# Normalised rows of the value stage transposed in 32 by 32 blocks on VectorE and kept by token tile, their residual added by an accumulating transfer

## The chip, the cores and the metric

The kernel runs on one core of a Trainium2 chip. The metric is the device time in microseconds of one execution.

The engines are TensorE (PE, matmuls; PEld is its weight load), VectorE (DVE), ScalarE (ACT), GpSimd (POOL) and SyncE (SP). SP issues the plain transfers between DRAM and the on-chip memory (SBUF); POOL issues those that add into what they write. Matmul results land in PSUM, which has eight banks.

## The reference

One layer of a streaming encoder over 2048 tokens of width 1024, all in float32. Each sub-layer normalises its input, and its output again before the residual sum:

```
u = rms_norm(h, g_mix_pre);   z = u @ w_in
y = concat(window_attention(z), gated_recurrence(z)) @ w_out
h = h + rms_norm(y, g_mix_post)
u = rms_norm(h, g_x_pre);     m = rms_norm(mem, g_mem)
y = cross_attention(u, m, wq_x, wk_x, wv_x) @ wo_x        # 4 heads, 256 memory tokens
h = h + rms_norm(y, g_x_post)
u = rms_norm(h, g_ffn_pre)
y = (silu(u @ w_gate) * (u @ w_up)) @ w_down              # inner width 2816
h = h + rms_norm(y, g_ffn_post)
```

The change is at the seam of the last two sub-layers: the second `h`, its norm, and the hand-over of `u` to the feed-forward.

## The kernel before

Float32 products are made of three passes in a rounded format: each operand is split into a high part (a copy by ACT, L997) and a low part (the rest, by DVE, L1000), and PE multiplies high by high, high by low and low by high (L1141 to L1143).

From about 740 us on the work is a list of jobs: the output projection (mixed stage), attention scores (score stage), values (value stage), gate and up projections for the first and the second 1024 tokens (feed-forward), and the down projection (down stage). Each job has blocks, each block two row tiles of 128 rows by 1024 columns of result. A block is done by Strassen's scheme in seven steps instead of eight; a step (`products`) is 12 matmuls of 128 by 128 by 512. Its moving operands are the T tiles: one for each of seven combinations of the weight's quarters, resident for a whole job, 128 by 2 (high, low) by 4 contraction tiles by 512. Seven slots hold them, so at the change from one job to the next each slot is refilled as its last user of the old job ends. Its stationary operands are the S tiles, formed for each block two steps ahead from `sraw` loads. In the feed-forward the roles are such that the activations `u` are the T tiles and the weights are streamed.

T tiles are made in halves by `resident`: a row tile is loaded, and `split2` writes its high and low parts. Where a combination of quarters is needed, it was formed before and stored to DRAM (`u0_s` for the first 1024 tokens, `u_s` for the second).

What follows a block's products is its tail, a generator (`after`) of which one piece runs with each step of the following blocks; the pieces are given in program order, and each engine works through its own queue in an order that a planner fixes at build time from simulated times. An engine that waits holds up all that is queued behind it. The mixed and score stages' tails hand their rows on by `blocked` and `store_blocked`: DVE transposes 32 by 32 blocks, and four stores put the quarters at their places in DRAM.

The value stage's tail (`value_block`, L1620) of the kernel before: root mean square of each row (ACT squares, POOL), scaling (L1640), the add of the `h1` rows that SP had loaded (L1644), the store of the sum, squares again (L1516), scaling (L1653); then `transposed` (L1394): eight PE transposes of 128 by 128 into two PSUM banks (L1402), copied out by ACT (L1403), and one store to `u_d`, which is laid out by contraction tile. For row tiles 4 to 7 the tiles 0 to 3 are read back and combined with them into `u0_s` by `token_sums` (L1441).

Of the kernel before, what the change touches and what calls it, by code (L numbers as in the profile page):

```python
# [18 lines left out]
P = 128  # L19
T = 2048  # L20
# [28 lines left out]
class Layer:  # L49
# [111 lines left out]
    def run(self):  # L161
# [13 lines left out]
        self.vo_d = tc.dram_tile([D, D], F32, name="vo_d")  # L175
        self.u_d = tc.dram_tile([KT, P, T], F32, name="u_d")
        self.h_d = tc.dram_tile([NFF, P, T], F32, name="hid_d")
# [288 lines left out]
    def in_first(self):  # L466
# [65 lines left out]
        def fetch():  # L532
            for s in range(2):
                for q in range(2):
# [11 lines left out]
                  for i, p in enumerate(self.ORDER)]  # L546
# [3 lines left out]
                      + [("v", lambda kind: iter([None]), out, after, keep) for _, out, after, keep in plain])  # L550
        phases = self.phases([(lambda i, j, a, n: raw[i, j][:, a:a + n, :], 4, blocks, None, {})], T)
        PE, ACT, DVE, POOL = (getattr(mybir.EngineType, e) for e in ("PE", "Activation", "DVE", "Pool"))
# [450 lines left out]

    def resident(self, get, nk, key, dst, keep, sums):

# [18 lines left out]
        def split(a, b, t, o):  # L1024
            if o is not None:
                nc.vector.tensor_tensor(t, t, o, ALU.add if key == 6 else ALU.subtract)
            self.split2(t, dst[:, 0, a:b], dst[:, 1, a:b], "A")

# [200 lines left out]
    def phases(self, jobs, first, prologue=None):  # L1229
# [51 lines left out]
        def half(g, tile):  # L1281

            if current[0] is None:
                if not queue:
                    return False
                free = min(slots, key=lambda s: s[1])
                if free[1] > g:
                    return False
                n, p, _ = k = queue.pop(0)
                slots.remove(free)  # L1290
                slots.append((free[0], uses[k][-1], free[2]))
                self._n += 1
# [5 lines left out]
                current[:] = [(k, self.resident(fetch(n, tile), jobs[n][1], p, dst, keep[n], jobs[n][3] is not None)), 0]  # L1298
            k, f = current[0]
# [52 lines left out]
        fresh = False  # L1352
        for _, nk, bl, _, beside in jobs:
            for i, (kind, _, out, follow, addend) in enumerate(bl):
# [86 lines left out]
    def token_sums(self, a, o, n):  # L1441
# [7 lines left out]
        for c, t in enumerate((a[:, 0:4], a[:, 4:8], o[:, 0:4], o[:, 4:8])):  # L1449
            self.store(self.u0_s[c].rearrange("p (k t) -> p k t", k=4)[:, :, n * P:(n + 1) * P], t)  # L1450
        yield

    def jobs(self):
# [7 lines left out]
        def ffn_u(b):  # L1461
            return lambda t, i, j, k0, n: self.load(
                t, self.u_d[4 * i + k0:4 * i + k0 + n, :, b * TB + j * 512:b * TB + (j + 1) * 512]
                .rearrange("k p t -> p k t"))

# [6 lines left out]
        def in_turn(*what):  # L1472
# [7 lines left out]
        d_s = [sums(f"d_s{c}", src, nk) for c, (src, _, nk) in enumerate(down)]  # L1480
        jobs = [(self.w_out, 4, kinds([self.mixed_block(n) for n in range(0, NT, 2)], 1), self.out_sums, {1: [qk_s[1]]}),
                (qk, 4, kinds([self.score_block(n) for n in range(0, NT, 2)]), qk_s[0], {1: [vo_s[1]]}),
                (vo, 4, kinds([self.value_block(n) for n in range(0, NT, 2)]), vo_s[0], {})]
        for b in range(NB):
            beside = {2: [in_turn(*(d[1] for d in d_s))]} if b else {4: [u_s[1]]}
            jobs.append((ffn_u(b), 4, kinds([blk for f in range(0, NFF, 2) for blk in self.hidden_blocks(b, f)], 0, "s"),
                         u_s[0] if b else self.u0_s, beside))
        for c, (src, f0, nk) in enumerate(down):
            jobs.append((src, nk, kinds([self.down_block(c, f0, nk, n) for n in range(0, NT, 2)], 0, "s"), d_s[c][0], {}))

# [129 lines left out]
    def value_block(self, n):  # L1620
# [14 lines left out]
        def after():  # L1635
            r = self.rstds(ss[0])
            s2 = self.small("q_s", 4)
            x = [self.rows_of(self.h1_d, n + i) for i in range(2)]
            for i in range(2):
                nc.vector.scalar_tensor_tensor(y[i], y[i], r[:, i:i + 1], self.g_x_post, ALU.mult, ALU.mult)  # L1640
            yield
            yield
            for i in range(2):
                nc.vector.tensor_tensor(y[i], y[i], x[i], ALU.add)  # L1644
                self.store((self.out if n < NT - 2 else self.h2_d)[(n + i) * P:(n + i + 1) * P, :], y[i])
                yield
# [154 lines left out]
```

## Time and profile before

| | us |
|---|---|
| median of 3 runs | 2549.66 |
| lowest, highest | 2549.39, 2551.5 |
| the profiled execution | 2550.57 |
| its span | 2548.9 |

Granted TensorE clock over the profiled execution: 0.997. The page gives busy time by engine; "A <- B" in a list of waits is the time that A sat idle until B ended, with how often and the longest. A group's row gives busy time and mean nanoseconds of one, then the idle time before it. Matmuls overlap, so the time of one is longer than the interval between two. Line numbers are those of the kernel before.

### The profile page before, as it was taken

The numbers are of one execution on the slowest core, as the hardware profiler recorded it, in microseconds if no ns is written. First come the engines' busy times: TensorE is split into PE (matmuls) and PEld (weight loads), VectorE is DVE, ScalarE is ACT, GpSimd is POOL, SyncE is SP. The second block draws the span as 40 slices with busy tenths as digits, with TensorE's granted clock in tenths as the row PEclk, the third lists the DMA queues.
The fourth block names the chain that finished last, engine by engine and source line by source line (L and its number), as shares of the span: only waits on it lengthen the run. The fifth ranks groups of instructions, "written<-read, shape, count | busy, mean of one in ns | idle before, by whom it ended". The sixth has DMA issues, their size and how long they took to land.

```text
span 2548.9 us, 34298 instructions
## 1 busy us (share of the span) xinstructions
PE 2506.6 (98%) x12006; PEld 2095.8 (82%) x12006; DVE 1797.3 (71%) x2871; ACT 1263.0 (50%) x2635; POOL 376.4 (15%) x540
## 2 busy tenths in 40 slices
PE   9999999999999999999999999999999999999998
PEld 8878888888997778878878888888888888888886
DVE  8885488986556889987876655576566557574766
ACT  5553467664565566566753333353333335443543
POOL 4231344321401112101200000000000000000022
PEclk9999999999999999999999999999999999999999
DMA  6455644773887896866964522254465434564776
GB/s 201 147 165 178 181 138 157 216 241 96 265 303 273 290 338 192 269 217 212 333 215 138 184 91 83 75 206 140 166 207 195 144 115 164 179 191 106 228 174 154
DMA packets 379437, 482.13 MB, mean 189 GB/s; under 512 B 22016, under 2 KB 274944, under 8 KB 379264
## 3 DMA queue, kind: packets, MB, share of 16 engines
q1 hardware_dynamic: 373216, 457.92, 55.1%
q0 software_dynamic: 6048, 22.02, 5.0%
q8 instruction: 94, 1.54, 0.2%
q14 instruction: 79, 0.65, 0.1%
HBM read 313.14 MB, written 166.72 MB: 188 GB/s over the span
## 4 chain that ended last, share of the span: by engine, by line
PE 81%; DVE 6%; DMA 5%; ACT 3%; issue 2%; POOL 1%; SPq 1%; DVEq 0%; POOLq 0%; ACTq 0%
PE psm L1141 22%; PE psm L1143 22%; PE psm L1142 22%; PE psg L158 2%; PE psg L156 2%; PE psg L157 2%; DVE S L1000 1%; DMA raw<-in_wv_x_dram 1%; DVE T L1000 1%; ACT junk L1516 1%; DMA sraw<-pt_d 0%; PE pss L1402 0%; PE pss L854 0%; SPq L75 0%; PE pst L854 0%
## 5 line engine op out<-in xcount | busy, mean ns | idle before, releaser
L1141 PE MATMUL psm<-T,S 128*128 128x512 f32 x2680 | 1034.8, 391 | 16.0 <-ACT part L1156 7.8
L1142 PE MATMUL psm<-T,S 128*128 128x512 f32 x2680 | 1043.3, 390 | 1.6 <-DVE T L1000 1.6
L1143 PE MATMUL psm<-T,S 128*128 128x512 f32 x2680 | 1030.6, 390 | 3.9 <-DVE S L1000 3.9
L1141 PEld LDWEIGHTS psm<-T,S 128*128 128x128 f32 x2680 | 503.6, 188 | 128.8 <-ACT part L1156 12.6
L1143 PEld LDWEIGHTS psm<-T,S 128*128 128x128 f32 x2680 | 503.8, 188 | 111.0 <-DVE S L1000 6.6
L1142 PEld LDWEIGHTS psm<-T,S 128*128 128x128 f32 x2680 | 503.9, 188 | 107.8 <-DVE T L1000 4.1
L997 ACT ACTIVATE S<-sum 128x512 fp32r<-128x512 f32 (+1 forms) x370 | 223.8, 619 | 370.0 <-PE psm L1143 268.0
L1000 DVE TENSOR_TENSOR S<-sraw,S 128x512 fp32r<-128x512 f32 (+1 forms) x315 | 211.4, 680 | 219.4 <-ACT S L997 216.4
L1156 ACT ACTIVATE part<-psm 128x512 f32<-128x512 f32 x285 | 168.4, 596 | 251.2 <-PE psm L1143 233.8
L1000 DVE TENSOR_TENSOR S<-sum,S 128x512 fp32r<-128x512 f32 (+1 forms) x388 | 257.6, 673 | 41.5 <-ACT S L997 37.7
L997 ACT ACTIVATE S<-sraw 128x512 fp32r<-128x512 f32 (+1 forms) x300 | 184.5, 617 | 107.6 <-PE psm L1143 101.9
L1549 POOL DMA_DIRECT2D y_d<-row x16 | 14.1, 879 | 1076.5 <-DVE row L1731 1025.6
L1000 DVE TENSOR_TENSOR T<-row,T 128x1024 fp32r<-128x1024 f32 (+1 forms) x112 | 130.9, 1184 | 27.7 <-ACT T L997 24.8
L156 PE MATMUL psg<-u,whi 128*128 128x512 f32 x320 | 127.7, 399 | 0.8 <-DVE z L728 0.8
L158 PE MATMUL psg<-u,wlo 128*128 128x512 f32 x320 | 127.6, 399 | 0.0
L157 PE MATMUL psg<-u,whi 128*128 128x512 f32 x320 | 127.0, 397 | 0.0
L1516 ACT ACTIVATE junk<-row 128x512 f32<-128x512 f32 x160 | 99.6, 624 | 45.3 <-DVE row L1538 21.7
L997 ACT ACTIVATE T<-row 128x1024 fp32r<-128x1024 f32 (+1 forms) x112 | 113.3, 1030 | 11.2 <-DMA row<-d_s 4.9
L1682 DVE TENSOR_TENSOR row<-psm,part 128x512 f32<-128x512 f32 x66 | 43.7, 687 | 66.5 <-PE psm L1143 66.5
L1691 DVE TENSOR_TENSOR part<-psm,part 128x512 f32<-128x512 f32 x66 | 43.8, 688 | 60.2 <-PE psm L1143 60.0
L1731 DVE TENSOR_TENSOR row<-psm,part 128x512 f32<-128x512 f32 x72 | 49.1, 688 | 49.5 <-PE psm L1143 49.4
L1000 DVE TENSOR_TENSOR wlo<-raw,whi 128x1024 fp32r<-128x1024 f32 x44 | 54.4, 1237 | 39.6 <-ACT whi L997 28.5
(362 smaller groups left out, 3591.5 us busy)
## 6 DMA issues: line engine op xcount, KB each, us to landing
sraw<-in_w_gate_dram SPq DMA_DIRECT2D x44, 512.0 KB, 3.6
sraw<-in_w_up_dram SPq DMA_DIRECT2D x44, 512.0 KB, 3.7
hid_d<-row SPq DMA_DIRECT2D x44, 512.0 KB, 2.6
sraw<-hid_d SPq DMA_DIRECT2D x32, 512.0 KB, 4.0
sraw<-in_w_in_dram SPq DMA_DIRECT2D x44, 256.0 KB, 3.8
z_d<-pair SPq DMA_DIRECT2D x20, 512.0 KB, 3.3
raw<-in_w_in_dram SPq DMA_DIRECT2D x20, 512.0 KB, 5.0
z_d<-z SPq DMA_DIRECT2D x20, 512.0 KB, 3.9
```

The costliest lines, as they stand in the source:

```text
L156: nc.tensor.matmul(ps, ah, bh, start=(i == 0), stop=False)
L157: nc.tensor.matmul(ps, ah, bl, start=False, stop=False)
L158: nc.tensor.matmul(ps, al, bh, start=False, stop=(i == n - 1))
L997: self.nc.scalar.activation(hi, raw, AF.Copy)
L1000: self.nc.vector.tensor_tensor(lo, raw, f32(hi), ALU.subtract)
L1141: nc.tensor.matmul(ps, s[:, 0, k, :], t[:, 0, k, :], start=st, stop=False, **kw)
L1142: nc.tensor.matmul(ps, s[:, 0, k, :], t[:, 1, k, :], start=False, stop=False, **kw)
L1143: nc.tensor.matmul(ps, s[:, 1, k, :], t[:, 0, k, :], start=False, stop=sp, **kw)
L1156: nc.scalar.activation(t, ps, AF.Copy)
L1516: self.nc.scalar.activation(junk, a, AF.Square, scale=float(D) ** -0.5, accum_out=to)
L1691: nc.vector.tensor_tensor(c, a, c, ALU.add)
L1731: nc.vector.tensor_tensor(d, a, b, ALU.add)
```

## The change

In the tail of the value stage:

- the residual rows of `h1` are no longer loaded by SP and added by DVE; POOL issues a transfer that adds them into the scaled row tile (`add`), and the store of the sum stands three steps behind it, one more than before;
- the PE transposes and the copies out of PSUM are replaced by two DVE block transposes for each row tile into a tile of its own, and by four stores instead of one;
- `u_d` is laid out by token tile, then half of the width, 128 partitions by 512;
- for the token sums all four row tiles of a block's two sums are read back from `u_d` (before, two of the four were still on chip), two steps ahead of their use.

In the feed-forward, the two halves of a T tile are now two groups of 256 tokens over all four contraction tiles (before: two contraction tiles over all 512 tokens). The splits read the tile through a view in runs of 32 elements; the number of instructions and of elements is the same. `u0_s` is written in rows of 512 elements instead of 128.

```diff
-        self.u_d = tc.dram_tile([KT, P, T], F32, name="u_d")
+        self.u_d = tc.dram_tile([NT, 2, P, 512], F32, name="u_d")
...
         def split(a, b, t, o):
             if o is not None:
                 nc.vector.tensor_tensor(t, t, o, ALU.add if key == 6 else ALU.subtract)
+            if bytoken:
+                t = t.rearrange("p n (a k c) -> p k (n a) c", a=4, k=4)
+                self.split2(t, *(dst[:, e, :, a * P:b * P].rearrange("p k (m c) -> p k m c", c=32) for e in range(2)),
+                            "A")
+                return
             self.split2(t, dst[:, 0, a:b], dst[:, 1, a:b], "A")
...
         for c, t in enumerate((a[:, 0:4], a[:, 4:8], o[:, 0:4], o[:, 4:8])):
-            self.store(self.u0_s[c].rearrange("p (k t) -> p k t", k=4)[:, :, n * P:(n + 1) * P], t)
+            self.store(self.u0_s[c, :, n * 512:(n + 1) * 512], t.rearrange("p k t -> p (k t)"))
...
         def ffn_u(b):
-            return lambda t, i, j, k0, n: self.load(
-                t, self.u_d[4 * i + k0:4 * i + k0 + n, :, b * TB + j * 512:b * TB + (j + 1) * 512]
-                .rearrange("k p t -> p k t"))
+            return lambda t, i, j, n0, n: self.load(
+                t, self.u_d[b * NPB + 4 * j + n0:b * NPB + 4 * j + n0 + n, i].rearrange("n p c -> p n c"))
...
         def after():
             r = self.rstds(ss[0])
             s2 = self.small("q_s", 4)
-            x = [self.rows_of(self.h1_d, n + i) for i in range(2)]
             for i in range(2):
                 nc.vector.scalar_tensor_tensor(y[i], y[i], r[:, i:i + 1], self.g_x_post, ALU.mult, ALU.mult)
-            yield
-            yield
+                self.add(y[i], self.h1_d, n + i)
+            for _ in range(3):
+                yield
             for i in range(2):
-                nc.vector.tensor_tensor(y[i], y[i], x[i], ALU.add)
                 self.store((self.out if n < NT - 2 else self.h2_d)[(n + i) * P:(n + i + 1) * P, :], y[i])
                 yield
...
             for i in range(2):
-                u[i] = self.transposed(y[i], y[i])
-                self.store_transposed(self.u_d, n + i, u[i])
-                if 4 <= n < 8:
-                    o[i] = self.row_tile().rearrange("p (k t) -> p k t", k=KT)
-                    self.load(o[i], self.u_d[:, :, (n - 4 + i) * P:(n - 3 + i) * P].rearrange("k p t -> p k t"))
+                self.store_blocked(self.u_d[n + i], self.blocked(y[i], self.row_tile()))
                 yield
-            if o:
-                yield
+            if 4 <= n < 8:
+                t = {}
+                for m in (n - 4, n, n - 3, n + 1):
+                    t[m] = self.row_tile()
+                    self.load(t[m].rearrange("p (h c) -> p h c", h=2), self.u_d[m].rearrange("h p c -> p h c"))
+                    t[m] = t[m].rearrange("p (k t) -> p k t", k=KT)
+                for _ in range(2):
+                    yield
                 for i in range(2):
-                    yield from self.token_sums(u[i], o[i], n - 4 + i)
+                    yield from self.token_sums(t[n + i], t[n - 4 + i], n - 4 + i)
```

The rest of the diff hands a flag (`bytoken`) from each job to `resident`; it is set for the two feed-forward jobs alone.

More of the change, by code (lines that the diff above doesn't have):

```diff
@@ L550, in in_first @@
                       + [("v", lambda kind: iter([None]), out, after, keep) for _, out, after, keep in plain])
-        phases = self.phases([(lambda i, j, a, n: raw[i, j][:, a:a + n, :], 4, blocks, None, {})], T)
+        phases = self.phases([(lambda i, j, a, n: raw[i, j][:, a:a + n, :], 4, blocks, None, {}, False)], T)
         PE, ACT, DVE, POOL = (getattr(mybir.EngineType, e) for e in ("PE", "Activation", "DVE", "Pool"))
@@ L1002, with resident @@
     CHAIN = (5, 7, 6, 4)
-    def resident(self, get, nk, key, dst, keep, sums):
+    def resident(self, get, nk, key, dst, keep, sums, bytoken):
         nc = self.nc
@@ L1297, in half @@
                 left[k] = 2
-                current[:] = [(k, self.resident(fetch(n, tile), jobs[n][1], p, dst, keep[n], jobs[n][3] is not None)), 0]
+                current[:] = [(k, self.resident(fetch(n, tile), jobs[n][1], p, dst, keep[n], jobs[n][3] is not None,
+                                                jobs[n][5])), 0]
             k, f = current[0]
@@ L1352, in phases @@
         fresh = False
-        for _, nk, bl, _, beside in jobs:
+        for _, nk, bl, _, beside, _ in jobs:
             for i, (kind, _, out, follow, addend) in enumerate(bl):
@@ L1480, in jobs @@
         d_s = [sums(f"d_s{c}", src, nk) for c, (src, _, nk) in enumerate(down)]
-        jobs = [(self.w_out, 4, kinds([self.mixed_block(n) for n in range(0, NT, 2)], 1), self.out_sums, {1: [qk_s[1]]}),
-                (qk, 4, kinds([self.score_block(n) for n in range(0, NT, 2)]), qk_s[0], {1: [vo_s[1]]}),
-                (vo, 4, kinds([self.value_block(n) for n in range(0, NT, 2)]), vo_s[0], {})]
+        jobs = [(self.w_out, 4, kinds([self.mixed_block(n) for n in range(0, NT, 2)], 1), self.out_sums, {1: [qk_s[1]]}, False),
+                (qk, 4, kinds([self.score_block(n) for n in range(0, NT, 2)]), qk_s[0], {1: [vo_s[1]]}, False),
+                (vo, 4, kinds([self.value_block(n) for n in range(0, NT, 2)]), vo_s[0], {}, False)]
         for b in range(NB):
@@ L1486, in jobs @@
             jobs.append((ffn_u(b), 4, kinds([blk for f in range(0, NFF, 2) for blk in self.hidden_blocks(b, f)], 0, "s"),
-                         u_s[0] if b else self.u0_s, beside))
+                         u_s[0] if b else self.u0_s, beside, True))
         for c, (src, f0, nk) in enumerate(down):
-            jobs.append((src, nk, kinds([self.down_block(c, f0, nk, n) for n in range(0, NT, 2)], 0, "s"), d_s[c][0], {}))
+            jobs.append((src, nk, kinds([self.down_block(c, f0, nk, n) for n in range(0, NT, 2)], 0, "s"), d_s[c][0], {}, False))
         return jobs
```

## The prediction

> **What bounds the kernel now.** I read the page first, for the share of each engine, then busy time by stretch, to see which engine is full in the stage that the change touches.
>
> ```profile
> span 2548.9 us, 34298 instructions
> ## 1 busy us (share of the span) xinstructions
> PE 2506.6 (98%) x12006; PEld 2095.8 (82%) x12006; DVE 1797.3 (71%) x2871; ACT 1263.0 (50%) x2635; POOL 376.4 (15%) x540
> ```
>
> ```profile
> 900.00:950.00 50.00, 50.00 (x223) 41.35 (x222) 42.21 (x51) 38.25 (x79) 10.97 (x21) 1.00 1.00 333
> 1050.00:1100.00 50.00, 50.00 (x223) 41.40 (x222) 46.28 (x88) 30.23 (x69) 5.76 (x11) 1.00 0.89 284
> 1160.00:1187.00 27.00, 27.00 (x133) 22.59 (x132) 20.91 (x28) 18.34 (x45) 3.80 (x6) 1.00 0.82 261
> 1214.00:1241.00 27.00, 27.00 (x132) 22.48 (x132) 24.75 (x32) 15.46 (x37) 7.09 (x9) 1.00 1.04 332
> 1350.00:1400.00 50.00, 50.00 (x222) 41.42 (x221) 32.50 (x49) 16.52 (x29) 0.00 (x0) 1.00 0.48 151
> 2430.00:2460.00 30.00, 30.00 (x134) 24.84 (x133) 16.16 (x23) 15.98 (x35) 5.75 (x9) 1.00 0.78 172
> ```
>
> The columns are the stretch and its length, busy time of PE, weight load, DVE, ACT and POOL, the granted clock, the share of the DMA engines and GB/s. The third and fourth rows lie in the value stage, whose tail is what changes; the fifth is the feed-forward stage after it, the last the down stage. PE is full in all of them at clock 1.00, so one matmul less is time less, as long as nothing else comes late. But DVE is busy for 24.75 of 27 us in the fourth row and the DMA engines are full there: little room for what the change puts on either. In the feed-forward stage both have plenty.
>
> **What the change removes from PE.** The value block's tail turns each normalised row tile with eight 128 by 128 transposes (L1402). PE in order of time around one such group:
>
> ```profile
> 1156.61 0.39 PE L1141 MATMUL psm<-T,S 128*128 128x512 f32 x1
> 1156.84 1.04 PE L1402 MATMUL pss<-ident,row 128*128 128x128 f32 x8
> 1157.63 0.48 PE L1142 MATMUL psm<-T,S 128*128 128x512 f32 x1
> 1157.94 0.39 PE L1143 MATMUL psm<-T,S 128*128 128x512 f32 x1
> 1158.17 0.40 PE L1141 MATMUL psm<-T,S 128*128 128x512 f32 x1
> ```
>
> From the start of the group (1156.84) to the second matmul behind it (1157.94) are 1.10 us, of which the first matmul would take 0.23 anyway (1157.94 to 1158.17). A group thus costs 0.87 us of PE. There are 16 row tiles, so 16 x 0.87 = 13.9 us of PE go. This is the largest term, and it is worth its full size only while PE stays fed.
>
> ```profile
> L1410 DVE STREAM_TRANSPOSE row<-row 128x512 f32<-128x512 f32 x64 | 40.4, 680 | 0.0
> ...
> L1644 DVE TENSOR_TENSOR row<-row,row 128x1024 f32<-128x1024 f32 x16 | 19.1, 1217 | 0.0
> ...
> L1403 ACT ACTIVATE row<-pss 128x512 f32<-128x512 f32 x32 | 17.3, 591 | 3.1 <-PE pss L1402 2.6 <-DVE part L1691 0.4
> ...
> L1402 PE MATMUL pss<-ident,row 128*128 128x128 f32 x128 | 16.6, 272 | 0.0
> ```
>
> **What DVE and ACT get.** On ACT, 32 copies out of PSUM go (17.3 us busy); nothing is added. On DVE, the 16 residual adds go, 19.1 us, and 32 block transposes come, the same shape as the 64 of the mixed and score stages: 32 x 40.4 / 64 = 20.2 us. DVE is therefore level, +1.1 us over the whole stage. Without the transposes the same DVE work has 13.9 us less to fit in: the fourth row's 24.75 of 27 becomes at most full where token sums fall. The score stage, the second row, ran DVE 46.28 of 50 with PE at 50.00 of 50, so a DVE at 93% need not hold PE up. I take +1 us, between 0 and +3.
>
> Here a rule speaks against the change. The Trainium skill, "VectorE: DVE Perf Modes", Rules for kernel authors, says to transpose 128 by 128 on TensorE where a PSUM destination will do. It counts one transpose by itself, and it would be right if DVE were the bound: then the removed PE time is worth nothing and the stage would get DVE's 1.1 us longer. In this trace PE is at 27.00 of 27 us and DVE at 20.91 in the third row, so PE's time decides there.
>
> What PE waits for in this stage, from 1106 to 1330 us:
>
> ```profile
> PE psm L1143 <- DVE S L1000: 2.5, 2, 1.4
> PE psm L1141 <- ACT part L1156: 2.0, 2, 1.5
> PE psm L1142 <- DVE T L1000: 1.6, 3, 0.8
> PE psm L1141 <- ACT S L997: 1.2, 1, 1.2
> PE psm L1141 <- DVE row L1538: 0.3, 1, 0.3
> ```
>
> ACT's part, 2.0 + 1.2 = 3.2 us, may shrink with ACT's relief; I don't count it, but it sets the best end: -13.9 - 3.2 = -17.1 us.
>
> **The residual rows by the accumulating transfer.** Two SP loads of h1 rows per block become two POOL transfers that add into the row tile. The down stage has such transfers:
>
> ```profile
> L1545 POOL DMA_DIRECT2D row<-y_d x12: 875/885/1234, 2407.2 to 2506.6; - x12
> ...
> DMA to landing us min/median/max: 5.3/8.0/9.5
> ```
>
> ```profile
> ACT junk L1516 <- DMA row<-y_d: 6.5, 6, 1.7
> ```
>
> An add that DVE did in 1.2 us now lands 8.0 us after an issue of 0.9. Behind it wait the store of the row (SP) and the mean squares on ACT; behind those, in ACT's own queue, the weight splits (L997) and the evictions (L1156) that PE needs. In the down stage ACT waited 6.5 us in all for 12 such transfers, and PE stayed at 30.00 of 30. How much room is there here?
>
> ```profile
> 1174.23 2.48 DVE L1640 SCALAR_TENSOR_TENSOR row<-row,q_r,g 128x1024 f32<-128x1024 f32 x2 [0.31 <-POOL q_r L1531]
> ...
> 1184.74 0.61 ACT L1516 ACTIVATE junk<-row 128x512 f32<-128x512 f32 x1
> ```
>
> ```profile
> L1640 DVE SCALAR_TENSOR_TENSOR row<-row,q_r,g x16: 1275/1280/1286, 1132.9 to 1281.7; 128x1024 f32<-128x1024 f32 x16
> ```
>
> The last row dates the stage: the scalings of the first block begin at 1132.9, the second of the last block's at 1281.7, so a block takes some 21 us and eight of them 170. From scaling to squares are 10.5 us, with one group of transposes in it (0.9), and the change puts the squares one step later. A step is 12 matmuls; at 222 in 50 us (the feed-forward row) that is 2.7 us. So 10.5 - 0.9 + 2.7 = 12.3 us. The first row is ready 1.24 (half of 2.48) + 0.9 + landing after the start, so landing may take 10.1 us; the second row, issued 1.2 later with its squares a step later, may take 11.6. Against 8.0, with 9.5 the longest, that holds, but the DMA engines are fuller here than in the down stage: 1.04 against 0.78, and 8.0 x 1.04 / 0.78 = 10.7. I take +1 us, with an upper end in the rival below. POOL is busy for 3.80 to 7.09 of 27 us; 16 issues x 0.9 = 14 us over the stage fit, and behind a waiting issue on POOL stands only the next block's reciprocal root.
>
> DMA work, from the page's queues:
>
> ```profile
> q1 hardware_dynamic: 373216, 457.92, 55.1%
> q0 software_dynamic: 6048, 22.02, 5.0%
> ```
>
> The plain queue moves 457.92 MB in 0.551 x 2548.9 = 1404 us, 1.61 us for a row tile of 0.524 MB; the accumulating queue 22.02 MB in 127 us, 3.03 us for the same. Sixteen rows cost 16 x 1.42 = 23 us more of all DMA engines, and the four extra row tiles read back for the token sums (8 loads for 4 before) 6 us. That is 29 us in a stage of 170, most of which must move into its gaps and into the feed-forward stage, at share 0.48. Rows and sums that are read ahead come later; that costs nothing until the T tiles of the feed-forward are late.
>
> **SP.** The 16 stores of the transposed rows become 64, of a quarter each, as the score stage issues them:
>
> ```profile
> L78 SPq DMA_DIRECT2D pt_d<-row x64: 303/467/1414, 979.8 to 1121.6; - x64
> ```
>
> That is 48 more issues at 0.47 = 23 us in the stage, less 16 loads. In the third and fourth block (row tiles 4 to 7) SP also waits for the stores before it reads the rows back, and behind it stand loads for the block after (21 us ahead), which covers it. The token sums come three steps, 8 us, later, in the fourth block; the T tiles that they feed are first used four blocks on. Nothing for either; if that cover is gone it comes out as the T rival.
>
> **T tiles in the feed-forward.** Halves are now split by token, not by contraction tile. Before, the first six matmuls of a product needed only one half; now each needs both. At the change of weights:
>
> ```profile
> 1298.12 0.40 PE L1143 MATMUL psm<-T,S 128*128 128x512 f32 x1
> 1298.52 0.50 PE L1141 MATMUL psm<-T,S 128*128 128x512 f32 x1
> 1299.78 0.50 PE L1142 MATMUL psm<-T,S 128*128 128x512 f32 x1 [0.76 <-DVE T L1000]
> ```
>
> Six matmuls had run while the second half was made; they would now wait, up to 6 x 0.225 = 1.35 us for a late tile. PE waited for T three times here (the list above), for two or so tiles: +2 us, between 0 and 7 x 1.35 = 9.5 if all seven are late. The reordered reading in the splits falls under the feed-forward row, where DVE is idle for 17.5 of 50 us: nothing.
>
> **Sum.** -13.9 + 1 + 1 + 2 = -9.9 us. The profiled execution took 2550.57 us and would become 2540.7; the median of the runs before is 2549.66, which gives 2539.8, so 2540.
>
> **Rivals.**
> (1) Slower: the accumulating transfers land too late. For it: the share of 1.04 and DMA work that grows by 29 us. Against: 8.0 us in a stage that is itself at 0.78, and the margin of 2 us or more. Price: in each of 8 blocks ACT stands for landing less 10.2 us, and PE behind it. At 12 us that is 8 x 1.8 = 14.4 us and eats all the gain: that is the deciding point. At 12.8 it is 20.8 - 13.9 = +6.9, some 2557. Chance 0.19.
> (2) No change: all seven T tiles are late, because row loads and token sums pile up at the end of the stage: -13.9 + 9.5 + 1 = -3.4, 2546. DVE as the bound (its +1.1, 2551) falls in the same class. For it: 24.75 of 27 us and full DMA engines. Against: the first and second rows above, where DMA at 1.00 or DVE at 93% left PE at 50.00. Chance 0.13.
> (3) Slower: descriptors of the POOL transfers are held up by DVE. In the down stage, with DVE about half busy, an issue took 885 ns and 1234 at most; with DVE at 90% an issue might wait until DVE pauses, say two steps (5.4 us) where the margin is 10.1 - 8.0 = 2.1; every block would lose 3.3 us at ACT: 8 x 3.3 - 13.9 = +12.5, 2562. This is the rule in the Trainium skill, "SBUF — State Buffer", SBUF: two separate sides: the GpSimd cores that write descriptors are locked out while a DVE instruction holds the port they share. No row here shows a longer hold than 0.35 us. Chance 0.03.
> (4) The order of queues that is built anew puts the tail's work in worse places, so that the change doesn't free PE: the 7.6 us that PE waits in the stage (the list above) grow by 19, +5, 2555. Nothing in the trace speaks for it but that every queue changes. Chance 0.03.
>
> **Numbers.** The forecast has 0.62. About 0.2% (5.1 us) is what this measurement can tell from no change: faster 0.62, same 0.13, slower 0.19 + 0.03 + 0.03 = 0.25. The range goes from the best end, 2549.66 - 17.1 = 2532.6, say 2533, to 2557, where rival (1) is at its price; past it lies the worse half of (1) and rival (3), under 2 in 10. The forecast's own range is 2533 to 2545.
>
> **What would show it.** Right: no transposes on PE, PE still full from 1160 on, the feed-forward's first output 10 us earlier, landing of the POOL transfers under 10 us, no more than a few us of ACT waiting for them. Wrong: ACT squares waiting for the row by 2 us or more in each block (rival 1), PE waiting for T L1000 by over 5 us (rival 2), POOL issues well over 0.9 us (rival 3).

## The result and the profile after

The changed kernel takes 2570.24 us (median of 6, 2566.67 to 2574.15), the kernel before in the same session 2549.52 (2546.95 to 2551.5): ratio 1.0089, 95% interval 1.0079 to 1.0099. It is slower, by 20.7 us on these medians and by 22.7 us as the ratio gives it (0.0089 of 2548 us, the measure used for all runs below), where 9.9 us less were forecast. The profiled execution took 2569.51 us.

The head of its page:

```profile
span 2567.8 us, 34068 instructions
## 1 busy us (share of the span) xinstructions
PE 2496.9 (97%) x11878; PEld 2083.1 (81%) x11878; DVE 1797.0 (70%) x2887; ACT 1247.1 (49%) x2603; POOL 375.4 (15%) x556
```

PE works 9.7 us less than before and DVE as long (1.1 us more were forecast), yet the span is 18.9 us longer. So PE waits more. Busy time by stretch (columns as before), first the kernel after, then three stretches of the kernel before that the prediction did not show:

```profile
1160.00:1187.00 27.00, 26.20 (x116) 21.36 (x115) 21.00 (x31) 16.05 (x40) 3.96 (x8) 1.00 0.88 230
1214.00:1241.00 27.00, 23.22 (x91) 17.67 (x90) 22.86 (x30) 11.46 (x28) 4.69 (x9) 0.94 0.91 275
1241.00:1268.00 27.00, 22.06 (x89) 17.76 (x88) 17.31 (x26) 8.23 (x18) 1.06 (x2) 0.87 1.05 317
1268.00:1295.00 27.00, 15.05 (x56) 11.28 (x54) 20.87 (x25) 18.47 (x40) 4.57 (x8) 0.81 1.02 315
1295.00:1322.00 27.00, 21.60 (x86) 17.07 (x87) 23.51 (x30) 16.74 (x28) 7.63 (x11) 0.93 1.01 317
```

```profile
1241.00:1268.00 27.00, 27.00 (x129) 22.52 (x128) 22.20 (x24) 20.95 (x44) 3.58 (x6) 1.00 0.92 327
1268.00:1295.00 27.00, 26.52 (x130) 21.82 (x129) 24.90 (x30) 20.73 (x37) 5.40 (x6) 1.00 1.04 363
1295.00:1322.00 27.00, 25.80 (x118) 20.24 (x117) 21.10 (x30) 16.77 (x32) 1.64 (x3) 1.00 0.46 153
```

Nearly all the loss lies between 1214 and 1322 us: the last four value blocks and the change of weights into the feed-forward. PE's clock falls there too, and the DMA engines, which before had room from 1295 on (0.46), are now full to 1322. From 1350 to 1400 PE is full again (50.00 of 50). The largest waits of PE from 1106 to 1349 us in the kernel after (7.6 us in all before):

```profile
PE psm L1146 <- ACT part L1161: 13.6, 7, 7.2
PE psm L1148 <- DVE S L1000: 6.9, 3, 4.9
PE psm L1146 <- ACT T L997: 6.4, 2, 3.6
PE psm L1147 <- DVE T L1000: 3.7, 2, 2.4
```

**How far ahead PE is.** The recorded high-by-low matmuls (L1142 before, L1147 after) count PE's progress. Their number up to a moment, less that of the kernel before, times the 3 matmuls of a set and 0.2265 us each, is a lead in us. It is counted here from 1130 us, where the value stage's tails begin, and good to some 2 us (counted over all three lines of a set, no entry moves by more); the labels are those of the experiments below.

| lead on the kernel before, us, at | 1220 | 1270 | 1310 | 1350 |
|---|---|---|---|---|
| after | +4.8 | -3.4 | -20.4 | -19.0 |
| x5, no transposes on PE, nothing in their place | +4.8 | +9.5 | +9.5 | +11.6 |
| e5, T halves by token alone | -2.0 | -0.7 | -6.8 | -6.8 |
| e2, accumulating residual alone | +0.7 | -1.4 | -9.5 | -9.5 |
| e6, after without the new tiles' read-back | +4.8 | +1.4 | -11.6 | -9.5 |
| e8, layout and halves, PE transposes | 0 | 0 | -8.8 | -7.5 |
| e11, e8 with 12 of 16 tiles by DVE | +2.7 | +4.1 | -8.2 | -6.1 |

In the first four blocks the change does gain, as forecast: +4.8 us by 1220. Then it loses 25 us in 90.

**Where the wait comes from.** The largest waits of ACT and DVE for DMA in the kernel after, 1215 to 1310 us:

```profile
ACT T L997 <- DMA row<-vo_d: 8.4, 1, 8.4
DVE sum L1121 <- DMA sraw<-in_w_gate_dram: 5.5, 1, 5.5
DVE row L1450 <- DMA row<-u_d: 5.0, 2, 4.7
ACT T L997 <- DMA row<-u_d: 4.6, 2, 2.5
ACT T L997 <- DMA row<-u_s: 4.6, 4, 2.4
```

In the kernel before the same stretch holds 2.1, 1.3 and 0.6 us. One instance in order of time, first DVE and then PE:

```profile
1253.75 0.69 DVE L1121 TENSOR_TENSOR sum<-sraw,sraw 128x512 f32<-128x512 f32 x1 [5.48 <-DMA sraw<-in_w_gate_dram]
...
1256.26 0.68 DVE L1000 TENSOR_TENSOR S<-sraw,S 128x512 fp32r<-128x512 f32 x1
```

```profile
1256.99 0.79 PE L1148 MATMUL psm<-T,S 128*128 128x512 f32 x1 [4.94 <-DVE S L1000]
1257.59 0.63 PE L1146 MATMUL psm<-T,S 128*128 128x512 f32 x1
1258.01 0.63 PE L1147 MATMUL psm<-T,S 128*128 128x512 f32 x1
```

DVE stands for 5.48 us before a sum of feed-forward weights, because their row is late. Behind it in DVE's queue stands the split of an S tile that PE needs for the present block, and PE stands for 4.94. Then the matmuls come 0.42 us apart (1257.59 to 1258.01) instead of 0.23, until 1261. The longest PE wait, 7.2 us for an eviction by ACT, has the same form: ACT had stood before T tiles whose rows were late (2.51 us for a `u_d` row within this wait), and the eviction was queued behind those.

The largest wait of the list, 8.4 us for a row of `vo_d`, shows two causes at once. SP's issue of the two last such rows, and the summary line of such loads from 1225 to 1260 us (its last number is the median time from issue to landing), before and then after:

```profile
1231.03 1.52 SPq L75 DMA_DIRECT2D row<-vo_d  x2
row<-vo_d SPq DMA_DIRECT2D x2, 512.0 KB, 7.2
```

```profile
1244.62 1.26 SPq L75 DMA_DIRECT2D row<-vo_d  x2
row<-vo_d SPq DMA_DIRECT2D x2, 512.0 KB, 12.5
```

The rows are issued 13.6 us later and take 5.3 us longer to land. In e1 below (no accumulating transfers) they are issued about as late, at 1240.5 and 1244.5, but land in 8.0 us. In e6 (new tiles not read back) they are issued at 1224.7 and 1235.3 and land in 7.7 us. In neither does ACT wait for them: in these traces it takes the late issue and the long landing together.

The DMA engines from 1215 to 1310 us (queue: packets, MB, share), before and then after:

```profile
q1 hardware_dynamic: 26087, 28.90, 88.6%
```

```profile
q1 hardware_dynamic: 17412, 24.76, 78.4%
q0 software_dynamic: 1062, 3.89, 21.3%
```

About the same bytes (28.90 and 28.65 MB) take 88.6% of the stretch before and 99.7% after. And the accumulating transfers themselves (kernel after, value stage):

```profile
L1550 POOL DMA_DIRECT2D row<-h_d x16: 865/901/1101, 1131.4 to 1301.2; - x16
...
  ACT junk L1521: 4.9, 4
...
DMA to landing us min/median/max: 5.0/7.8/11.5
```

Their issue takes 0.90 us and ACT waits 4.9 us for them in all (the landings are of all 28 transfers of this line). Rivals (1) and (3) as priced did not happen. The late T tiles of rival (2) did (PE waits 6.4 + 3.7 = 10.1 us for T), but not at the price it was given.

### The profile page after: what moved, and what is told of

It reads as the page before. It is cut to its first block, busy times and chain, and to the rows that moved or that the text cites. A ratio compares the mean times of both kernels' runs of the same rounds, so it can differ in the third digit from the quotient of the medians.

```text
span 2567.8 us, 34068 instructions
## 1 busy us (share of the span) xinstructions
PE 2496.9 (97%) x11878; PEld 2083.1 (81%) x11878; DVE 1797.0 (70%) x2887; ACT 1247.1 (49%) x2603; POOL 375.4 (15%) x556
## 4 chain that ended last, share of the span: by engine, by line
PE 75%; DVE 9%; DMA 8%; issue 3%; ACT 3%; POOL 1%; SPq 1%; DVEq 0%; POOLq 0%; ACTq 0%
PE psm L1146 20%; PE psm L1148 20%; PE psm L1147 20%; PE psg L158 2%; PE psg L157 2%; PE psg L156 2%; DVE S L1000 1%; DVE T L1000 1%; DMA row<-u_d 1%; DMA g<-vo_d 1%; DVE row L1416 1%; SPq L75 1%; DVE sum L1121 1%; DMA sraw<-in_w_gate_dram 1%; DMA raw<-in_wv_x_dram 0%
## 5 line engine op out<-in xcount | busy, mean ns | idle before, releaser
L1147 PE MATMUL psm<-T,S 128*128 128x512 f32 x2680 | 1044.7, 390 | 3.7 <-DVE T L1000 3.7
L1147 PEld LDWEIGHTS psm<-T,S 128*128 128x128 f32 x2680 | 504.9, 188 | 110.5 <-DVE T L1000 6.3
L1554 POOL DMA_DIRECT2D y_d<-row x16 | 13.9, 871 | 1079.6 <-DVE row L1737 1017.5
```

The costliest lines, as they stand in the source:

```text
L1147: nc.tensor.matmul(ps, s[:, 0, k, :], t[:, 1, k, :], start=False, stop=False, **kw)
```

## The experiments

Two families of theory stood at the start. **A**: the residual's accumulating transfer costs, because SP's stores wait for it ahead of other loads (**A1**) or because it takes more of the DMA engines (**A2**). **B**: the side that makes the T tiles costs, by the read-back of the new row tiles for the token sums (**B1**), or by DVE being full at the change of weights and the halves by token (**B2**). Where a ratio is given in us, it is its distance from 1 times 2548. The queue orders are planned anew for each run, so a run shows its part together with its own order; a worse order as such (rival (4)) is not separated by any of them.

### e1 and e2: the residual undone, and the residual alone

e1 is the kernel after with the residual as before; e2 is the kernel before with the residual of the kernel after:

```
e1:  -  self.add(y[i], self.h1_d, n + i)
     +  x = rows_of(self.h1_d, ...); two steps later: y[i] += x[i] on DVE
e2:  the same lines the other way round, in the kernel before
```

> The changed kernel with the residual as it was: SP loads the h1 rows, DVE adds them, same steps as before; block transposes, layout by token and token sums stay as changed. Before is 2549.5 us, the changed kernel 2570.2. Theory A (the accumulating transfers cost the time, by the SP queue or by DMA capacity): the loss goes, 2540 to 2552, the upper end if DVE, which now has the adds and the transposes, holds PE up. Theory B (the token sums' read-back or the T halves by token cost the time): still 2560 or more.

> The kernel before with the residual edit alone: POOL's accumulating transfers and the store a step later; PE transposes and the old layout stay. Theory A: slower than before by the loss without the gain of the transposes, 2565 to 2585. Theory B: within 3 us of before, or faster, since DVE loses 19 us of adds.

Measured: e1 2565.34, ratio 1.0061 [1.0044, 1.0078]; e2 2559.84, ratio 1.0041 [1.0026, 1.0056]. Alone the accumulating transfers, with the store a step later, cost 10.4 us; taken out of the changed kernel they give back 7.1. Neither family is the whole: without them 15.5 us of loss stay.

### e3 and e4: SP's queue

```
e3:  the store of the sum moved behind the second squares
e4:  the store issued from ACT's queue, right behind each tile's squares
```

> The changed kernel with the store of the sum issued by SP two to three steps later, behind the second squares, so that the transfer has landed when SP comes to the store. In the changed kernel SP stood 44 us at six such stores, 12.3 us at one. Theory A1 (SP's queue held up, and the loads behind it late): 2545 to 2560. Theory A2 (DMA capacity: the accumulating transfers take 3 us of all engines each) and theory B: 2565 to 2573.

> The changed kernel with the store of the sum issued from ACT's queue behind the squares of its row, which wait for the same transfer anyway; SP never waits for an accumulating transfer. Theory A1: 2540 to 2556, lower than with the later store. Theory A2 and theory B: 2565 to 2575.

Measured: e3 2569.25, ratio 1.0081 [1.0066, 1.0097]; e4 2578.69, ratio 1.0120 [1.0104, 1.0135]. e3 did not do what it was made for. SP issues the stores at the same times in it as in the kernel after (the third block's first at 1180.13 us in both), and stands as long in front of them: 45.4 us in six waits in e3, and in the kernel after, from 1130 to 1340 us:

```profile
SPq L78 <- DMA row<-h_d: 44.4, 6, 12.3
```

e4 takes this wait from SP, but ACT then stands 16.2 us for the same rows, and the kernel is slower. So neither is a clean test of A1. What speaks against A1 is the place: 40.9 of the 44.4 us lie before 1205 us, where the change gains; between 1205 and 1260 us, where the loss begins, SP stands 3.5 us so, and after that not at all. A1 is unlikely, but no run excludes it.

### e6 and e9: the read-back of the new tiles

e6 is the kernel after with the token sums formed from the blocked tile still on chip (its token sums are then not those of the reference; four loads fewer). e9 leaves nothing out: tiles 4 to 7 go by PE, with ACT's copy writing the new layout, so that the sums use the tiles on chip; the other 12 by DVE.

```
e6:  -  load(t[n], u_d[n])                  +  t[n] = the blocked tile on chip
e9:  +  if 4 <= n < 8: transposed_blocked(y) (PE, ACT)  else: blocked(y) (DVE)
```

> The changed kernel without reading the new row tiles back for the token sums: the sums take the block-transposed tile as it lies on chip, whose quarters stand in other partitions than the sums need, so those sums are not the reference's; four of eight loads go, the number of sums and stores stays. Theory B1 (the read-back makes the token sums late, SP, DVE and the T tiles wait for them): 2550 to 2560. Theory B2 (DVE full at the change of weights, or the T halves by token): 2565 to 2572.

> The changed kernel, but row tiles 4 to 7 are transposed by PE so that the token sums need no read-back of the new tiles; the other 12 tiles by DVE, residual by the accumulating transfers. 12 x 0.87 = 10.4 us of PE time would still be saved. Theory B1: the late loss mostly goes, 2543 to 2556, the upper end if the accumulating transfers cost what they cost alone (11 us). Theory B2: 2562 or more.

Measured: e6 2562.65, ratio 1.0059 [1.0044, 1.0074]; e9 2557.31, ratio 1.0042 [1.0027, 1.0057]. Four loads and the wait for them are worth 7.6 us (1.0089 to 1.0059). In the lead table e6 still has +1.4 at 1270, where the kernel after has lost it. By e6, B1 holds for about a third of the loss. e9 gives back more, 12.0 us (1.0089 to 1.0042), though PE has four groups to do again.

### e8 and e11: the layout without DVE's transposes, and with them

e8 has the new layout and halves, but PE transposes, sums from the tiles on chip and the residual as before. e11 is e9 with the residual as before, so it differs from e8 in 12 row tiles moved from PE to DVE.

```
e8:   all tiles: transposed_blocked(y) (PE, ACT);  residual by SP and DVE
e11:  if 4 <= n < 8: transposed_blocked(y)  else: blocked(y);  residual by SP and DVE
```

> The new layout alone: token-tile layout of the transposed rows, T halves by token, contiguous sums; but PE transposes (the ACT copy puts the elements at their new places, one store of whole rows), sums from tiles on chip, and the residual by SP and DVE as before. If the T halves by token cost the time (B2, halves): 2553 to 2563. Otherwise within 3 us of before, 2546 to 2551.

> As the run with PE transposes for row tiles 4 to 7, and the residual by SP loads and DVE adds as before. Theory B1: the best of all, 2540 to 2548, if DVE (12 tiles of block transposes, 15 us more than before) does not become the bound. If DVE is the bound at the change of weights: 2552 to 2562.

Measured: e8 2556.09, ratio 1.0033 [1.0019, 1.0046]; e11 2557.72, ratio 1.0041 [1.0026, 1.0056]. The layout with its halves costs 8.4 us by itself. Twelve groups of transposes fewer on PE, 10.4 us by the prediction's price, bring nothing that can be measured (+2.0, the intervals overlap): the lead table shows +4.1 at 1270 and -8.2 at 1310.

e9 and e11 differ in the residual alone, and lose 10.7 and 10.4 us: beside these sums the accumulating transfers cost nothing that can be measured, against 10.4 us in the kernel before and 7.1 in the changed one. So the parts do not simply add; what the transfers cost depends on what else is late. The share of the DMA engines does not decide it either: from 1215 to 1310 us it is 98.9% in e9 and 89.8% in e11.

### e5: the halves alone

The kernel before, old layout, but halves by token:

```
-  get(4 contraction tiles k0..k0+2, 512 tokens)    +  get(4 contraction tiles, 256 tokens)
```

> The kernel before, with the T tiles of the feed-forward split into halves by token instead of by contraction tile; everything else as before, but the rows come in packets of 1 KB instead of 2 KB. The prediction's term: +2 us, 2548 to 2550. If the halves by token are what the version with layout alone lost at the change of weights (PE 7 us ahead until 1270, level at 1310): 2552 to 2557, with PE waiting for T from ACT and DVE by 5 us or more between 1280 and 1310. If the loss lay in the token sums or in the accumulating transfers: within 2 us of before.

Measured: 2557.46, ratio 1.0031 [1.0018, 1.0044], +7.9 us: nearly all of e8's loss. PE and ACT of e5 at the change of weights:

```profile
1283.90 0.39 PE L1147 MATMUL psm<-T,S 128*128 128x512 f32 x1
1289.65 1.22 PE L1145 MATMUL psm<-T,S 128*128 128x512 f32 x2 [5.36 <-ACT T L997]
1290.67 0.63 PE L1146 MATMUL psm<-T,S 128*128 128x512 f32 x1
1291.10 0.63 PE L1147 MATMUL psm<-T,S 128*128 128x512 f32 x1
```

```profile
1286.72 1.28 ACT L1690 ACT_TABLE_LOAD   x1 [1.77 <-DVE row L1688]
1288.02 0.63 ACT L1690 ACTIVATE row<-row 128x512 f32<-128x512 f32 x1
1288.55 1.04 ACT L997 ACTIVATE T<-row 128x1024 fp32r<-128x1024 f32 x1
```

In ACT's queue the second half of the T tile stands behind the first feed-forward block's silu (L1690), which waits for DVE and loads its function table. In the kernel before, the same silu and table load stand in ACT's queue (1292.90 us, after 2.61 us of waiting) and PE runs on; now PE stands for 5.36 us and then runs at half rate. e8, which has the same halves, shows the same wait of 5.36 us for a T tile from ACT (1286.81).

### x5: PE's transposes alone

The kernel before; ACT copies the row tile to itself in place of PE's transposes and the copies out of PSUM. It leaves the transposition out.

```
-  ps = bank; 4 x nc.tensor.transpose(ps, y);  tv <- ps (ACT)
+  tv <- y (ACT)
```

> The kernel before, with the 128 by 128 transposes of the value blocks left out: ACT copies the normalised row tile to the transposed tile's place, in the same halves, so ACT, DVE, SP and the DMAs keep their work and only PE loses the 16 groups. It leaves out the transposition itself. The prediction's term by itself (16 x 0.87 us of PE, all of it shortening the whole): 2546 - 13.9 = 2532 to 2536. If the change of weights into the feed-forward (1270 to 1310) is paced by the queues of ACT and DVE and by the row loads, and not by PE, PE runs ahead and waits there: 2540 to 2548, with PE ahead of before by 7 us or more at 1250 and by less than half of that at 1320.

Measured: 2540.45, ratio 0.9969 [0.9956, 0.9981], -7.9 us. So 7.9 of the 13.9 us are real (4.8 to 11.2 by the interval). The time lies in the range of the second theory, but its sign did not come: x5 is 7.5 us ahead at 1250, 9.5 at 1270, 5.4 at 1290 and 9.5 again at 1310. Stretches of 20 us, x5 and then the kernel before:

```profile
1190.00:1210.00 20.00, 17.62 (x71) 14.09 (x70) 17.05 (x26) 11.58 (x29) 7.59 (x6) 0.91 1.06 336
...
1270.00:1290.00 20.00, 16.81 (x67) 12.14 (x67) 19.68 (x24) 14.27 (x27) 1.54 (x3) 1.00 0.87 306
1290.00:1310.00 20.00, 20.00 (x90) 16.56 (x89) 14.68 (x23) 9.24 (x17) 0.00 (x0) 1.00 0.53 162
```

```profile
1270.00:1290.00 20.00, 20.00 (x97) 16.38 (x95) 17.90 (x20) 16.43 (x28) 4.80 (x6) 1.00 1.02 359
1290.00:1310.00 20.00, 18.32 (x80) 13.93 (x80) 17.98 (x24) 13.91 (x26) 1.64 (x3) 1.00 0.51 182
```

A full stretch of x5 holds 90 matmuls. From 1190 to 1210 it holds 71: PE waits 2.38 us for DVE's S split, again with half rate behind it (the kernel before has 1.42 us of this wait, and no half rate), and the lead falls from 5.4 us at 1200 to 2.0 at 1210. From 1270 to 1290 x5 holds 67, with DVE at 19.68 of 20 us, but then 90 where the kernel before holds 80, eight of them transposes: the kernel before has its own slow stretch there, and x5 loses nothing to it in the end. The traced execution (2537.01 us) is the fastest of five, so its lead of 11.6 us is above what the median shows. Why the median gains less stays open.

### x7 and x8: only some of the tiles to DVE

Tiles 0 to 7 as before, with the old layout and halves for the first 1024 tokens; the residual as before. x7 moves tiles 8 to 15 to DVE, x8 only 8 to 11.

```
+  if n < 8: as before   elif n >= 12 (x8 only): transposed_blocked(y)   else: blocked(y)
```

> The block transposes on DVE for row tiles 8 to 15 alone, kept by token tile; tiles 0 to 7, which the first feed-forward half and the token sums read, go as before (PE, old layout, T halves by contraction tile, sums from the tiles on chip); the residual as before (SP load and DVE add). PE loses 8 groups, 7.0 us; DVE gains 16 transposes, 10 us, all of it from 1205 on. If the token halves and the late sums at the change of weights ate the gain, this keeps it: 2540 to 2543. If PE's lead is lost at the change of weights whatever feeds it: 2546 to 2549. If DVE is the bound there (full from 1281 on), its 2 x 1.3 us a block come out: 2549 to 2555.

> As the version that moves tiles 8 to 15 to DVE, but only tiles 8 to 11, so that the last two blocks before the change of weights keep PE's transposes and give DVE nothing more to do there; halves by token in the second feed-forward half alone. PE loses 4 groups, 3.5 us. By the gain that PE's transposes alone showed (7.8 of 13.9): -2 us, 2546 less or so. If PE's lead is lost at the change of weights whatever feeds it, or by the token halves of the second feed-forward half (PE 48.2 of 50 us at 1700 to 1750): 0 to +2 us.

Measured: x7 2546.96, ratio 0.9997 [0.9988, 1.0006]; x8 2547.72, ratio 1.0000 [0.9991, 1.0009]. No change in either. Both keep the old halves for the first 1024 tokens, and the loss that e5 and e8 have at the change of weights is gone. Counted as in the lead table x8 is 4.8 us ahead at 1270, 0.7 at 1290 and 1.4 at 1350, though the blocks there have no more work on DVE than in the kernel before. Its stretch:

```profile
1270.00:1290.00 20.00, 17.40 (x82) 13.49 (x81) 20.00 (x24) 12.81 (x21) 2.27 (x3) 1.00 1.04 357
```

DVE is busy for 20.00 of 20 us (17.90 before) and the DMA share is 1.04 (1.02 before): PE comes earlier and finds DVE full. This fits the lost lead but is argued from one trace: the drop is 3 to 4 us with a count good to 2, and x5's lead comes back at the same place. From 1700 to 1750 us, where the halves by token of the second 1024 tokens come in, x8 also does 211 matmuls where the kernel before does 217, another 1.4 us.

### x1, e12 and e13: the transfers' share of the DMA engines

x1 adds accumulating transfers to the kernel before that nobody waits for; e12 and e13 are e2 in the first five or the last three value blocks alone.

```
x1:   +  nc.gpsimd.dma_start(y_d[...], h1_d[...], accum_op=add)    (2 a row tile)
e12:  acc = n < 10        e13:  acc = n >= 10
```

> The kernel before, with accumulating transfers added that nobody waits for: at each scaling of a value row tile POOL issues two of 128 by 512 that add the h1 rows into a scratch array in DRAM (32 transfers, 8.4 MB in all). The loads of the residual and its add on DVE stay. It tests the share of the DMA engines by itself. If the loss is one of DMA capacity before the change of weights (row loads land late because the accumulating transfers take their time): 2555 to 2562, with loads of u_s and vo_d rows landing after 10 us or more between 1230 and 1290. If it is the work on ACT's and DVE's queues and the late token sums: within 3 us of before.

Measured: 2571.73, ratio 1.0090 [1.0075, 1.0105]. It tested another place than was meant: nothing tied the transfers to the scalings, and POOL's order put them into the mixed stage. There they cost 23 us, but POOL itself stood 93.6 us in its queue until the rows were stored, so that the run does not separate DMA share from POOL's queue. It is left out of the reasons below.

> The kernel before, with the residual by the accumulating transfer in the first five value blocks alone (row tiles 0 to 9); the last three as before. If the accumulating transfers cost in every block (a later row, ACT's squares behind it, the evictions behind those): 5/8 of the 10 us that they cost in all blocks, 2553 to 2556, and the scalings of the second and third block already come later than before. If they cost only at the change of weights, where row loads, DVE and ACT are full: within 2 us of before.

> The kernel before, with the residual by the accumulating transfer in the last three value blocks alone (row tiles 10 to 15). If the cost is the same in every block: 3/8 of 10 us, 2551 to 2553. If it lies at the change of weights: 2555 to 2559, with the last scaling 10 us or more later after the first than before (160 against 147.6 us) and waits of ACT for u_s rows of 5 us or more.

Measured: e12 2552.36, ratio 1.0021 [1.0012, 1.0029], +5.3 us; e13 2551.51, ratio 1.0015 [1.0006, 1.0023], +3.8 us. The total splits by the number of blocks, but not for the reason that "cost in every block" gave: up to 1230 e12 has lost nothing against before (lead 0.0). It loses 2.7 us at 1230 to 1240, and 3.4 more at 1280 to 1290, after its last accumulating block. The first of these, on DVE in e12:

```profile
1231.28 0.69 DVE L1444 TENSOR_TENSOR row<-row 128x512 f32<-128x512 f32 x1 [4.77 <-DMA u_d<-row]
...
1234.07 0.68 DVE L1000 TENSOR_TENSOR S<-sum,S 128x512 fp32r<-128x512 f32 x1
```

The token sums work in place on a tile that is being stored to `u_d`. This store lands some 9 us after SP issued it (1222.17), DVE stands 4.77 us for it, the S split for PE is queued behind, and PE stands for that split 1.89 us at 1235.41. In the kernel before the same sum does not wait; two others do, for 2.05 and 1.32 us, with landings of some 6 us. The DMA share from 1220 to 1230 is near 1 in both (1.01, before 0.96), but the engines stay full longer in e12: 1.07 from 1250 to 1270, before 0.87. So the transfers cost later than where they stand, through row loads and stores in the queues of DVE and ACT. Whether it is their share of the DMA engines (A2) or the tail that stands a step later in e2, e12 and e13 is not separated: a run that loads the DMA engines at this place and nothing else is lacking, since x1 missed it.

**Where the residual and the read-back meet.** Both make the token sums late. SP's stores of `u0_s` (`u_s` in the profile) end at 1239 us in the kernel before and between 1227 and 1237 in e5, e8, e11, e13, x5, x7 and x8. In the runs with the accumulating transfers in the blocks that form the sums they end at 1257 (e2), 1261 (e12), 1255 (e9), 1263 (e6) and 1268 (after); with the read-back and no such transfers (e1) at 1261. The first loads of these rows for the T tiles come later too, from 1253 (e9) to 1273 (after) where the kernel before has 1249. In e2, ACT's wait for them and PE's wait behind it, from 1130 to 1350 us:

```profile
ACT T L997 <- DMA row<-u_s: 7.4, 3, 3.1
PE psm L1141 <- ACT part L1156: 8.7, 2, 7.9
```

ACT stands for the rows between 1264 and 1275; the eviction that PE needs follows in its queue at 1285.84, and PE stands 7.9 us for it. In the kernel before ACT waits for no such row. That the two parts reach PE by the same late rows fits that they do not add. It is not the only way: e13, whose transfers come after these blocks, still loses 3.8 us.

## Why the prediction was wrong, by its steps

| step | forecast, us | runs |
|---|---|---|
| 16 groups leave PE | -13.9 | -7.9 (x5) |
| T halves by token | +2 (0 to 9.5) | +7.9 (e5) |
| accumulating residual | +1 | +10.4 alone (e2), +7.1 in the whole (e1), +0.3 beside PE's sums (e9 less e11) |
| token sums late, rows read back | 0 | +7.6 in the whole (e6) |
| DVE level | +1 | not alone; with 12 groups off PE together +2.0 (e11 less e8) |

The three measured alone and the read-back in the whole make -7.9 + 7.9 + 10.4 + 7.6 = 18.0; the ratio of the whole is 22.7. This account does not close and need not: the parts do not add (the residual costs 10.4, 7.1 or 0.3 us by what stands beside it), each interval is 3 us or more either way, and DVE's 32 transposes have no run of their own.

**The removed PE time.** Its size, 0.87 us a group, held where PE stayed fed: at 1190 us, after four groups (3.5 us), x5 is 4.1 ahead. The step that failed is "worth its full size only while PE stays fed", which the stretch 1160 to 1187 was taken to secure for the whole stage: 7.9 of 13.9 us came out. In x5 PE stands behind DVE at 1204 already. Where DVE does the transposes instead, no gain is left (e11 less e8, x7, x8); that PE then waits at the change of weights, where DVE is full, is argued from x8.

**The halves.** The mechanism was named rightly: both halves are now needed before a product. Its price, six matmuls or 1.35 us a tile, was the wrong quantity. What counts is how much later the second half stands in ACT's queue: behind the silu, 5.36 us once (e5 and e8), and half rate after it.

**The residual.** Landing was priced where the row is waited for, ACT's squares; that held (4.9 us in all). The step that failed is the 29 us of extra DMA work "most of which must move into its gaps", with rows and sums that come later, put at nothing "until the T tiles of the feed-forward are late". They were late: with the transfers alone (e2) the stores of the sums end at 1257 us instead of 1239, ACT stands 7.4 us for rows that it did not wait for before, and PE 7.9 us for an eviction behind them. Whether the share of the DMA engines or the later step of the tail makes them late stays open, as does why beside PE's sums (e9) the transfers cost nothing, though the stores end at 1255.

**The token sums.** "Nothing for either", said of SP and of the sums, failed. The sums were to come 8 us later. The stores of `u0_s` ended at about 1239 us before and at 1264 to 1268 after, and the loads of their rows were issued from 1249 before and from 1272 after. SP's waits for the read-back were to be covered by loads that stand 21 us ahead; the rows of `vo_d` were issued 13.6 us later than before, and in e6, without the read-back of the new tiles, at 1224.7 and 1235.3 (e12 issues them late without it, at 1240.3 and 1243.5, so it is not the only way). The case "if that cover is gone it comes out as the T rival" is what happened, but rival (2) had given that rival a price that only ate the gain.

**The rule on transposes.** Twelve row tiles moved from PE to DVE brought nothing (e11 less e8, +2.0 us), though PE did gain at 1160 us, where the prediction weighed the rule. The Trainium skill, "VectorE: DVE Perf Modes", Rules for kernel authors, prefers TensorE for 128 by 128. The outcome agrees with it; why the gain is lost is not shown.

What held: no transposes left on PE, the gain in the first four blocks, DVE's total (1797.0 against 1797.3), POOL's issue time, ACT's small wait for the transfers. Two of its signs of being right did not come: PE was not quite full from 1160 on (26.20 of 27 us), and the longest landing was 11.5 us, not under 10. What SP's 48 extra issues cost by themselves no run shows.

## What to carry to other kernels

Time freed on a full engine need not come out whole, because the next full place may not let it through: look for that place at the seam behind the changed stage, where the new job's buffers are filled, and price it with that stretch's rows, not with those of the steady state. A late transfer costs where an in-order queue stands before it, so ask what is queued behind each instruction that waits for a DMA, not only who wants the row. A row can be late by its issue or by its landing: read both, in the queue that issues it and in the time to landing. Test a sum of small terms part by part: here three that had been put at +1, +2 and 0 cost 10.4, 7.9 and 7.6 us in runs of their own. And test them in pairs, since they need not add.

## What the runs showed of the hardware

A PE wait of about 2 us can cost more than itself. After waits of 1.89 (e12), 2.38 (x5), 2.22, 4.94 and 7.23 us (after) and 5.36 us (e5) the next six to nine matmuls start 0.43 us apart instead of 0.23, some 8 x 0.2 = 1.6 us more, and the granted clock is low there; after 1.42 us (before), 1.95 (e13), 2.69 (e6, at 1207 us) and 3.61 (after, at 1310.63 us) they do not. So the length of the wait alone does not decide it. From the longest wait of the kernel after:

```profile
1295.48:1299.00 3.52, 3.52 (x9) 2.80 (x10) 2.01 (x2) 3.28 (x4) 2.54 (x4) 0.56 1.06 364
```

The Trainium skill, "TensorE: Matmul & The Clock Gate", Part 1, gives 426.7 ns for such a matmul at half clock, which agrees; it puts the fall of the clock after an idle window of about 3.4 us, and here it followed waits of 1.9 to 2.4 us too, and did not follow one of 3.61 us.

An accumulating transfer takes more of the DMA engines than a plain one, in the full stretch too: 21.3% of 95 us for 3.89 MB is 5.2 us a MB, against 78.4% for 24.76 MB, 3.0 us a MB, in the same 95 us.
